# One gathered pair in fp32, fourteen early weight slots, and expert outputs fetched back by row index

## Chip, cores and metric

The kernel runs on one core of a Trainium2 chip. The metric is device microseconds of that core. The kernel is fp32 throughout: a sequence of 512 tokens of width 1024 goes through one layer, a hybrid mixer and then a mixture of experts.

## What is computed

The mixer (short convolution, sparse attention, gated delta rule) is not touched by the change; what matters is that its result `x + mixer(...)`, called x1 here, is the input of the expert stage. Of that stage the reference says, in short:

```python
lg = xt @ w_rg + b_rg                      # 4 groups
grp = argmax(lg); p_grp = softmax(lg)[grp]
le = (xt @ w_re + b_re)[group grp]         # 8 experts in the group
top_p, top_i = top_k(softmax(le), 2)
gate = top_p / sum(top_p) * p_grp
expert = grp * 8 + top_i                   # 2 of 32 experts for each token
y = (silu(xb @ w_eg[e]) * (xb @ w_eu[e])) @ w_ed[e]    # for every expert's tokens xb
x = x1 + sum over a token's two experts of gate * y
```

`xt` is the normalised x1. An expert has three matrices of 1024 x 512 or 512 x 1024 in fp32, 2 MB each, and 512 tokens make 1,024 assignments, 32 for an expert on average. The kernel gives each expert 64 slots (`CAP`) and has a slow loop behind the main part for experts with more.

## The kernel before

Tokens lie in four tiles of 128 (`NT`), x1 in the tiles `x1p`. The order of the instructions on each engine is fixed when the program is built: a planner simulates the program and orders it by when things are ready; each engine's queue then runs in that order, with semaphores for the waits. Only the tags of tiles (which buffer is used again by what) and a few `issue_after` bounds are written by hand.

**The end of the mixer, lines 854 to 1022.** The product with `w_out` is made in column blocks: three quarters of the columns first (L864 to L874, sums in `acc` and `acc2`, added to x1 at L908 and L910), the last quarter tile by tile in the loop of L965 (products L973 to L975, added at L979). In the same loop each tile is routed: squares on ScalarE (L926), mean on VectorE (L984), the power -1/2 on GpSimd (L985), logits from transposed x1 (L940), and then a chain of some 17 short operations on VectorE (L1004 to L1018) that finds the group, the two experts and the mask `asg`. `slots_of` counts each token's place in its expert by a product with a triangular matrix (L961) and `choose` (L954) turns the places into a one-hot matrix `pm0`: token by slot, for the four experts of pairs 0 and 1.

**Pairs of experts.** The expert stage goes over 16 pairs; pair p holds experts p and p + 16, with 64 slots each, so 128 slots. The inputs of a pair are `xT`, 128 slots turned and scaled by the norm's gain. There are two ways to get it. For pairs 0 and 1 the tokens are gathered by TensorE: x1 is split into a rounded part `h2h` and a rest `h2l` (`parts`, a cast on VectorE at L921 and a subtraction on GpSimd at L922), and both are multiplied with the one-hot columns (`gather_t`, L1092 and L1093; 64 products of 256 columns), and the sums in four PSUM banks are scaled in 16 operations (L1129). The slots' token number, norm and gates come from another product (L1123) into `info0`. For pairs 2 to 15 `next_input` reads rows of x1 from device memory by an indirect DMA from GpSimd (L1137, out-of-range slots skipped), and TensorE turns them (L1144). The row indices `tix` come from a table written by eight indirect DMAs (L1064), read back by eight DMAs on ScalarE's queue (L1100) and summed at L1102.

**Weights.** `wchunk` (L1079) loads weights in pieces of 128 x 2048 fp32, 1.049 MB, on SyncE's queue (L1085), 12 a pair: four for the gate and up halves of each expert, two for its down half. A piece goes into the next of 18 slots in rotation, and its load waits until the slot's last user is done. The first 11 slots (`wslots`, L854) are free before the mixer ends; their loads are bound behind the loads of the mixer's last weights. The other seven (L1075, L1076) are the operand tiles of the `w_out` product, `hTh` and `hTl`, and the three tiles that held `h2h` and part of `h2l`.

**A pair's work.** `ffn_up` makes gate and up products for one expert (L1162 and L1163, side by side in the two column halves of the array), then silu and gating (L1173, L1174) and four transposes (L1180, copied at L1181). `ffn_down` makes the down products (L1206). What happens to the output depends on the pair:

- Pairs 0, 2, ..., 12 (`by_rows`, L1260): the output is copied and scattered by an indirect DMA into `yrows` in device memory (L1215), at the row of its token, choice 1 and choice 2 apart. `yrows` was zeroed long before.
- The other pairs: the output is split in two parts (L1195, L1196) and combined by products with a one-hot matrix `sel` (L1240, 16 products a pair), whose sums are added to x1 on VectorE (L1242). These steps are strewn into the next pair's products (`combine_step`).

`add_rows` (L1223), called in pair 14, reads `yrows` back in eight plain DMAs of 0.5 MB on GpSimd's queue (L1227) and adds each to x1 (L1229). Its tiles `yr` share two buffers (`ringa`, tag `raw`) with the rows `xg` of `next_input`. The last expert's down half is loaded and combined in three column pieces (L1297 to L1313), each followed by the stores of these columns.

Of the kernel before, what the change touches and what calls it, by code (L numbers as in the profile page):

```python
# [11 lines left out]
F32 = mybir.dt.float32  # L12
# [87 lines left out]
def kernel(ctx, tc, x, w_in, w_nat, w_small, w_gate, w_branch, w_out, cmp_w1, cmp_w2,  # L100
# [753 lines left out]
    wslots = [(lp, "yg"), (mp, "es0"), (mp, "es1"), (lp, "nq"), (lp, "nkv")] + [(mp, f"es{i}") for i in range(2, 8)]  # L854
# [37 lines left out]
    tg = mp.tile([P, NT, 2, 4], F32, name="tg")  # L892
# [6 lines left out]
    G.tensor_copy(ti[:, :, 0], C("tokm"))  # L899
    for i in range(2):  # L900
        G.tensor_copy(inf[:, :, i, 0], C("tokm"))
        G.tensor_copy(tg[:, :, i, 0], C("tokm"))
        G.tensor_scalar(out=inf[:, :, i, 3], in0=C("tokm"), scalar1=float(S * i), scalar2=None, op0=ALU.add)
# [11 lines left out]
    def turned(ap, cols):
        return ap.rearrange("p (k q) -> p k q", k=KT)[:, :, cols.start // KT:cols.stop // KT]

    def parts(t, cols):
        x1 = x1p[t // 2][:, t % 2, cols].rearrange("p (q k) -> p k q", k=KT)
        hi, lo = turned(h2h[t // 2][:, t % 2], cols), turned(h2l[t], cols)  # L920
        V.tensor_copy(hi, x1)  # L921
        G.tensor_tensor(out=lo, in0=x1, in1=hi.bitcast(F32), op=ALU.subtract)  # L922
# [21 lines left out]
    for t in range(NT):  # L944
# [3 lines left out]
        parts(t, c3[0])  # L948
    pm0 = [lp.tile([P, 2, 4, CAP], F32R, tag=f, name="pm0") for f in ("fa", "fb")]


    def choose(pm, t):
        for b in range(2):
            V.tensor_tensor(out=pm[t // 2][:, t % 2, 2 * b:2 * b + 2],  # L954
                            in0=iota[:, 1:1 + CAP].unsqueeze(1).to_broadcast([P, 2, CAP]),
                            in1=pos[:, t, b::16].unsqueeze(2).to_broadcast([P, 2, CAP]), op=ALU.is_equal)
# [8 lines left out]
    for t in range(NT):  # L965
# [53 lines left out]
        parts(t, c3[1])  # L1019
# [18 lines left out]
    A.activation(exs, exs, AF.Exp)  # L1038
    V.tensor_reduce(out=se, in_=ex, axis=AX.X, op=ALU.add)
# [36 lines left out]
    slots += [(lp, "yhi"), (lp, "ylo"), (mp, "h2lp")]  # L1076
# [13 lines left out]

    def gather_t(px, k, t, sel, start, stop):
        T.matmul(px, h2h[t // 2][:, t % 2, k * P:(k + 1) * P], sel, start=start, stop=False)  # L1092
        T.matmul(px, h2l[t][:, k * P:(k + 1) * P], sel, start=False, stop=stop)  # L1093
# [331 lines left out]
```

## Time and profile before

| what | value |
|---|---|
| median of 3 runs (lowest, highest) | 1220.06 us (1218.9, 1220.84) |
| the profiled execution: time | 1220.9 us |
| the profiled execution: span | 1219.1 us |
| mean granted TensorE clock | 0.965 |
| PE, DVE, ACT, POOL busy | 91%, 48%, 27%, 10% of the span |
| moved by DMA | 274.81 MB, mean 225 GB/s |

The profile shows one execution on the chip. PE is TensorE's products, PEld its weight loads, DVE VectorE, ACT ScalarE, POOL GpSimd, SP SyncE; an engine's name with a q is its queue, which issues DMAs. L1162 is line 1162 of the kernel before. A row of a timeline has start and duration in us, engine and line, operation, the output and inputs by their names in the program, and a count where neighbours are merged; in square brackets stands how long the engine had been idle before it, and what ended that. A row of a list of waits has the sum, the number and the longest. Matrix products are pipelined, so a busy PE need not be at its peak. What a product costs is read from the distance between starts.

### The profile page before, as it was taken

To read this page: it belongs to the slowest core of one execution; us is meant where nothing else is said; L and a number is where in the kernel's file an instruction comes from. 1 tells how busy PE (TensorE), PEld (TensorE's weight loads), DVE (VectorE), ACT (ScalarE), POOL (GpSimd) and SP (SyncE) were. 2 spreads that over 40 slices of the span, in tenths; PEclk is the share of its full clock that TensorE was granted. 3 is DMA by queue.
4 is the path that set the end of the run, shared out by engine and by line. 5 is a ranking of instruction groups with operands and counts; after the bars stand their busy time and mean duration, and the time that the engine had idled before them with its cause. 6 is when DMAs were issued, how large, how long until landed. Compare 5 with 4: busy or idle time off the path is not lost. (4 is left out here: it accounts for less than half of the span.)

```text
span 1219.1 us, 15948 instructions
## 1 busy us (share of the span) xinstructions
PE 1115.0 (91%) x6167; PEld 717.7 (59%) x6168; DVE 590.3 (48%) x1406; ACT 332.3 (27%) x640; POOL 117.1 (10%) x172
## 2 busy tenths in 40 slices
PE   0899999999999999999999889997997989797985
PEld 0788798987788887766889833433332323232333
DVE  1586585586544775564445842414141414141356
ACT  1434343343332544566234201010110101010110
POOL 3100220410010000000002431000010000000000
PEclk9899999999999999999999889999998989898997
DMA  8133233212213221200781679999999999999953
GB/s 328 56 101 90 70 104 124 93 62 87 70 53 114 87 71 51 55 16 13 257 328 74 242 274 418 420 418 419 419 418 420 420 420 419 419 419 418 412 215 122
DMA packets 53488, 274.81 MB, mean 225 GB/s; under 512 B 8500, under 2 KB 12468, under 8 KB 28576
## 3 DMA queue, kind: packets, MB, share of 16 engines
q1 hardware_dynamic: 44928, 254.95, 53.8%
q0 software_dynamic: 5328, 14.33, 3.1%
q10 hardware_dynamic: 3152, 4.45, 1.0%
q8 instruction: 50, 0.82, 0.3%
q14 instruction: 30, 0.25, 0.1%
HBM read 266.73 MB, written 12.34 MB: 229 GB/s over the span
## 5 line engine op out<-in xcount | busy, mean ns | idle before, releaser
L1162 PE MATMUL pgu<-we,xT 128*64 128x512 f32 x512 | 245.1, 627 | 37.8 <-DMA we<-in_w_eg_dram 29.1
L1163 PE MATMUL pgu<-we,xT 128*64 128x512 f32 x512 | 240.6, 619 | 4.5 <-DMA we<-in_w_eu_dram 4.4
L189 PE MATMUL pmm<-hTh,lo 128*128 128x512 f32 x432 | 172.0, 398 | 0.2 <-DVE lo L182 0.2
L187 PE MATMUL pmm<-hTh,hi 128*128 128x512 f32 x432 | 171.2, 396 | 0.0
L188 PE MATMUL pmm<-hTl,hi 128*128 128x512 f32 x432 | 170.9, 395 | 0.0
L182 DVE TENSOR_TENSOR lo<-raw,hi 128x1024 fp32r<-128x1024 f32 x82 | 100.9, 1231 | 115.6 <-ACT hi L181 113.3
L1162 PEld LDWEIGHTS pgu<-we,xT 128*64 128x64 f32 x512 | 69.8, 143 | 130.2 <-issue 105.9
L181 ACT CAST hi<-raw 128x1024 fp32r<-128x1024 f32 x82 | 86.1, 1050 | 165.5 <-PE pmm L188 94.9
L1206 PE MATMUL pd<-we,aT 128*64 128x512 f32 x496 | 122.3, 598 | 0.5 <-DVE aT L1181 0.5
L1163 PEld LDWEIGHTS pgu<-we,xT 128*64 128x64 f32 x512 | 69.5, 142 | 63.2 <-issue 48.8
L1173 ACT ACTIVATE act<-pgu,rss 64x512 f32<-64x512 f32 x32 | 21.8, 681 | 274.0 <-PE pgu L1163 181.4
L189 PEld LDWEIGHTS pmm<-hTh,lo 128*128 128x128 f32 x432 | 81.6, 189 | 17.9 <-DVE lo L182 1.8
L187 PEld LDWEIGHTS pmm<-hTh,hi 128*128 128x128 f32 x432 | 81.8, 189 | 16.6 <-DVE fa L704 0.6
L188 PEld LDWEIGHTS pmm<-hTl,hi 128*128 128x128 f32 x432 | 81.6, 189 | 16.5
L1174 DVE SCALAR_TENSOR_TENSOR act<-pgu,gsl,act 64x512 f32<-64x512 f32 x32 | 24.2, 757 | 128.0 <-ACT act L1173 127.7
L1181 DVE COPY aT<-pt 128x256 f32<-128x256 f32 x32 | 13.5, 423 | 127.8 <-PE pt L1180 127.8
L1206 PEld LDWEIGHTS pd<-we,aT 128*64 128x64 f32 x496 | 35.5, 136 | 60.8 <-issue 56.1
L1240 PE MATMUL pc<-y,sel 128*128 128x512 f32 (+2 forms) x152 | 51.6, 450 | 10.5 <-DVE x L1242 6.4
L1242 DVE TENSOR_TENSOR x<-pc,x 128x512 f32<-128x512 f32 (+2 forms) x76 | 46.0, 656 | 22.4 <-PE pc L1240 21.8
L1240 PEld LDWEIGHTS pc<-y,sel 128*128 128x128 f32 x152 | 26.3, 198 | 44.5 <-DVE y L1196 14.4
L1195 ACT CAST y<-pd 64x512 fp32r<-64x512 f32 (+2 forms) x40 | 21.2, 537 | 104.5 <-PE pd L1206 53.6
L1215 POOL DMA_INDIRECT yrows<-yd,yix x14 | 14.2, 1013 | 274.6 <-ACT yd L1214 266.8
(794 smaller groups left out, 1849.4 us busy)
## 6 DMA issues: line engine op xcount, KB each, us to landing
we<-in_w_eg_dram SPq DMA_DIRECT2D x64, 1024.0 KB, 20.6
we<-in_w_eu_dram SPq DMA_DIRECT2D x64, 1024.0 KB, 20.0
we<-in_w_ed_dram SPq DMA_DIRECT2D x62, 1024.0 KB, 20.9
raw<-in_w_in_dram SPq DMA_DIRECT2D x30, 512.0 KB, 3.5
raw<-in_w_gate_dram SPq DMA_DIRECT2D x24, 512.0 KB, 3.5
raw<-in_w_branch_dram SPq DMA_DIRECT2D x12, 512.0 KB, 3.5
yrows<-zero POOLq DMA_DIRECT2D x1, 4096.0 KB, 21.7
raw<-in_w_nat_dram SPq DMA_DIRECT2D x8, 512.0 KB, 4.1
```

The lines of the kernel that those rows point to most:

```text
L181: A.copy(out=hi, in_=raw)
L182: V.tensor_tensor(out=lo, in0=raw, in1=hi.bitcast(F32), op=ALU.subtract)
L187: T.matmul(ps, ahi(k), bhi(k), start=start and k == 0, stop=False)
L188: T.matmul(ps, ahi(k), blo(k), start=False, stop=False)
L189: T.matmul(ps, alo(k), bhi(k), start=False, stop=stop and k == n - 1)
L1162: T.matmul(pgu[0:64], xs(k), wg(k), start=k == 0, stop=k == KT - 1)
L1163: ins = T.matmul(pgu[64:128], xs(k), wu(k), start=k == 0, stop=k == KT - 1)
L1173: A.activation(at, qk(pgu[0:64]), AF.Silu, scale=rss[0:64])
L1174: V.scalar_tensor_tensor(out=at, in0=qk(pgu[64:128]), scalar=gsl[64:128], in1=at, op0=ALU.mult, op1=ALU.mult)
L1206: T.matmul(pd[64 * a:64 * a + 64], aT[:, k], wd(k, a), start=k == 0, stop=k == 3)
L1240: T.matmul(pc[:, 0:n], sel[:, t * P:(t + 1) * P], y[:, cols], start=i == 0, stop=i == len(src) - 1)
L1242: V.tensor_tensor(out=xo, in0=pc[:, 0:n], in1=xo, op=ALU.add)
```

## The change

1. **Gather.** Only pair 0 is gathered by TensorE, and in fp32 straight from x1: 32 products of 128 columns, no split. `parts` and its buffers `h2h`, `h2l`, `h2lp` go; the squares are written to a plain tile `sq`; `choose` and `tg` cover two experts in place of four. The sums lie in two PSUM banks; one is scaled by one VectorE operation, the other by four on ScalarE. The slots' information for pair 0 is made inside pair 0's first up half (`first_info`). Pair 1's rows are now fetched by `next_input` like the others'.
2. **Slots.** `h2lp` is gone, and a tile `es8` of the same size is added. It and the tiles `yhi` and `ylo`, used before by `h2h`, are now among the early slots: 14 early ones in place of 11, and 18 in all as before.
3. **Outputs.** Pairs 0 to 6 are scattered in place of 0, 2, ..., 12; pairs 7 to 15 are combined by products. `add_rows` is called in pair 8. It computes row indices, sets assignments to later pairs out of range, and fetches `yrows` by eight indirect DMAs into zeroed tiles.
4. The activation table for silu is loaded once behind the exponentials of the routing.

```diff
-    wslots = [...] + [(mp, f"es{i}") for i in range(2, 8)]
+    wslots = [...] + [(mp, f"es{i}") for i in range(2, 9)]
+    wslots += [(lp, "yhi"), (lp, "ylo")]
...
-    h2h = [lp.tile([P, 2, D], F32R, tag=t, name="h2h") for t in ("yhi", "ylo")]
-    h2l = [ringa.tile([P, D], F32R, tag="raw", name="h2l", bufs=2) for _ in range(2)]
-    h2lp = mp.tile([P, 2, D], F32R, tag="h2lp", name="h2lp")
-    h2l += [h2lp[:, t] for t in range(2)]
+    sq = ringa.tile([P, D], F32, tag="raw", name="sq", bufs=2)
...
-        A.activation(turned(h2l[t], cols), x1.rearrange("p (q k) -> p k q", k=KT), AF.Square, accum_out=ss)
+        A.activation(sq[:, cols], x1p[t // 2][:, t % 2, cols], AF.Square, accum_out=ss)
...
-        parts(t, c3[0])
-    pm0 = [lp.tile([P, 2, 4, CAP], F32R, tag=f, name="pm0") for f in ("fa", "fb")]
+    pm0 = [lp.tile([P, 2, 2, CAP], F32, tag=f, name="pm0") for f in ("fa", "fb")]
...
-        for b in range(2):
-            V.tensor_tensor(out=pm[t // 2][:, t % 2, 2 * b:2 * b + 2],
...
+        V.tensor_tensor(out=pm[t // 2][:, t % 2], in0=iota[:, 1:1 + CAP].unsqueeze(1).to_broadcast([P, 2, CAP]),
+                        in1=pos[:, t, 0::16].unsqueeze(2).to_broadcast([P, 2, CAP]), op=ALU.is_equal)
...
-        parts(t, c3[1])
...
+    A.activation(sc[:, 63:64], mhalf, AF.Silu)
...
-    slots += [(lp, "yhi"), (lp, "ylo"), (mp, "h2lp")]
...
+    row2 = lambda t: pm0[t // 2][:, t % 2].rearrange("p e s -> p (e s)")
+    pxs = [mpsum(n).rearrange("p (i n) -> p i n", i=4) for n in ("pgu", "pd")]
     for t in range(NT):
         for k in range(KT):
-            gather_t(pxs[k // 2][:, k % 2], k, t, row4(pm0, t), t == 0 and k % 2 == 0, t == NT - 1 and k % 2 == 1)
...
-    inputs = [pair_input() for _ in range(2)]
-    for b, xT in enumerate(inputs):
-        for k in range(KT):
-            V.tensor_scalar(out=xT[:, k], in0=pxs[k // 2][:, k % 2, P * b:P * b + P], scalar1=gain[:, k:k + 1],
-                            scalar2=None, op0=ALU.mult)
+            T.matmul(pxs[k // 4][:, k % 4], x1p[t // 2][:, t % 2, k::KT], row2(t), start=t == 0 and k % 4 == 0,
+                     stop=t == NT - 1 and k % 4 == 3)
+    inputs = [pair_input()]
+    V.tensor_tensor(out=inputs[0][:, 0:4], in0=pxs[0], in1=gain[:, 0:4].unsqueeze(2).to_broadcast([P, 4, P]), op=ALU.mult)
+    for k in range(4, KT):
+        A.activation(inputs[0][:, k], pxs[1][:, k - 4], AF.Copy, scale=gain[:, k:k + 1])
+    info0 = mp.tile([P, 4], F32, name="info0")
+
+    def first_info(h):
+        if h == 0:
+            pi = ps_e.tile([P, 4], F32, tag="pt", name="pi")
+            for t in range(NT):
+                T.matmul(pi, row2(t), tg[:, t], start=t == 0, stop=t == NT - 1)
+            V.tensor_copy(info0, pi)
+        return slot_info(info0, slice(64 * h, 64 * h + 64), 2 + h)
...
-        if pair < 4:
+        if pair < 3:
             G.memset(xg, 0.0)
...
     def add_rows():
+        rix = mp.tile([P, NT, 2], I32, name="rix")
+        V.tensor_scalar(out=half, in0=at_e, scalar1=float(by_rows), scalar2=4096.0, op0=ALU.is_ge, op1=ALU.mult)
+        V.scalar_tensor_tensor(out=half, in0=half, scalar=4096.0, in1=over, op0=ALU.add, op1=ALU.add)
+        V.tensor_tensor(out=rix, in0=half, in1=inf[:, :, :, 3], op=ALU.add)
         for i in range(2):
             for t in range(NT):
                 yr = ringa.tile([P, D], F32, tag="raw", name="yr", bufs=2)
-                G.dma_start(yr, yrows[2 * S * i + 2 * P * t:2 * S * i + 2 * P * t + 2 * P].rearrange("(p a) n -> p (a n)", a=2))
+                G.memset(yr, 0.0)
+                G.indirect_dma_start(out=yr, out_offset=None, in_=yrows.rearrange("(r a) n -> r (a n)", a=2),
+                                     in_offset=bass.IndirectOffsetOnAxis(ap=rix[:, t, i:i + 1], axis=0),
+                                     bounds_check=2 * S - 1, oob_is_err=False)
                 x1 = x1p[t // 2][:, t % 2]
                 V.tensor_tensor(out=x1, in0=yr, in1=x1, op=ALU.add)
...
-    by_rows = range(0, 14, 2)
...
-                     None if h else up[1][0], yix[:, h, pair:pair + 1] if pair in by_rows else None)
+                     None if h else up[1][0], yix[:, h, pair:pair + 1] if pair < by_rows else None)
...
-            if h == 0 and pair == by_rows[-1] + 2:
+            if h == 0 and pair == by_rows + 1:
                 add_rows()
```

More of the change, by code (lines that the diff above doesn't have):

```diff
@@ L851 @@
     branch(1, yhi, ylo)
-    wslots = [(lp, "yg"), (mp, "es0"), (mp, "es1"), (lp, "nq"), (lp, "nkv")] + [(mp, f"es{i}") for i in range(2, 8)]
+    wslots = [(lp, "yg"), (mp, "es0"), (mp, "es1"), (lp, "nq"), (lp, "nkv")] + [(mp, f"es{i}") for i in range(2, 9)]
+    wslots += [(lp, "yhi"), (lp, "ylo")]
     m_hi, m_lo = quarters("hTh", F32R), quarters("hTl", F32R)
@@ L891 @@
     inf = mp.tile([P, NT, 2, 4], F32, name="inf")
-    tg = mp.tile([P, NT, 2, 4], F32, name="tg")
+    tg = mp.tile([P, NT, 4], F32, name="tg")
     exi = mp.tile([P, NT, 2], F32, name="exi")
@@ L899 @@
     G.tensor_copy(ti[:, :, 0], C("tokm"))
+    G.tensor_copy(tg[:, :, 0], C("tokm"))
     for i in range(2):
         G.tensor_copy(inf[:, :, i, 0], C("tokm"))
-        G.tensor_copy(tg[:, :, i, 0], C("tokm"))
         G.tensor_scalar(out=inf[:, :, i, 3], in0=C("tokm"), scalar1=float(S * i), scalar2=None, op0=ALU.add)
@@ L913 @@
     c3 = slice(0, 768), slice(768, 1024)
[L915 to L922, printed above, removed]
     def squares(t, cols, ss):
-        x1 = x1p[t // 2][:, t % 2, cols]
-        A.activation(turned(h2l[t], cols), x1.rearrange("p (q k) -> p k q", k=KT), AF.Square, accum_out=ss)
+        A.activation(sq[:, cols], x1p[t // 2][:, t % 2, cols], AF.Square, accum_out=ss)
     x1T = [None] * NT
@@ L1046 @@
     V.tensor_tensor(out=oh[0], in0=oh[0], in1=oh[1], op=ALU.add)
+    G.tensor_copy(tg[:, :, 1], rs4)
+    G.tensor_copy(tg[:, :, 2:4], oh[0][:, :, 0::16])
     G.tensor_copy(ti[:, :, 1], rs4)
@@ L1089 @@
     gain = PR("nffg")
-    def gather_t(px, k, t, sel, start, stop):
-        T.matmul(px, h2h[t // 2][:, t % 2, k * P:(k + 1) * P], sel, start=start, stop=False)
-        T.matmul(px, h2l[t][:, k * P:(k + 1) * P], sel, start=False, stop=stop)
     def pair_input():
@@ L1111 @@
                             scalar2=8192.0 + a, op0=ALU.mult, op1=ALU.add)
-    row4 = lambda pm, t: pm[t // 2][:, t % 2].rearrange("p e s -> p (e s)")
-    pxs = [mpsum("pgu") for _ in range(2)] + [mpsum("pd") for _ in range(2)]
-    pxs = [px.rearrange("p (i n) -> p i n", i=2) for px in pxs]
+    row2 = lambda t: pm0[t // 2][:, t % 2].rearrange("p e s -> p (e s)")
+    pxs = [mpsum(n).rearrange("p (i n) -> p i n", i=4) for n in ("pgu", "pd")]
     for t in range(NT):
         for k in range(KT):
-            gather_t(pxs[k // 2][:, k % 2], k, t, row4(pm0, t), t == 0 and k % 2 == 0, t == NT - 1 and k % 2 == 1)
-    pi = ps_e.tile([P, 2, 4], F32, tag="pt", name="pi")
-    for b in range(2):
-        for t in range(NT):
-            T.matmul(pi[:, b], row4(pm0, t)[:, P * b:P * b + P].bitcast(F32), tg[:, t, b], start=t == 0, stop=t == NT - 1)
-    info0 = mp.tile([P, 2, 4], F32, name="info0")
-    V.tensor_copy(info0, pi)
-    inputs = [pair_input() for _ in range(2)]
-    for b, xT in enumerate(inputs):
-        for k in range(KT):
-            V.tensor_scalar(out=xT[:, k], in0=pxs[k // 2][:, k % 2, P * b:P * b + P], scalar1=gain[:, k:k + 1],
-                            scalar2=None, op0=ALU.mult)
+            T.matmul(pxs[k // 4][:, k % 4], x1p[t // 2][:, t % 2, k::KT], row2(t), start=t == 0 and k % 4 == 0,
[12 more added lines that the diff above has]
+        return slot_info(info0, slice(64 * h, 64 * h + 64), 2 + h)
     def next_input(pair):
         xg = ringa.tile([P, D], F32, tag="raw", name="xg", bufs=2)
-        if pair < 4:
+        if pair < 3:
             G.memset(xg, 0.0)
@@ L1266 @@
             up.append(ffn_up(lambda k: xT[:, k, es], *weights_up(w_eg[e], w_eu[e]),
-                             lambda: slot_info(info0[:, pair], es, 2 + h) if pair < 2 else slot_info(info[:, pair], es),
+                             lambda: slot_info(info[:, pair], es) if pair else first_info(h),
                              up[0][0] if up else None))
```

5 lines of the change are left out of this document (1 added, 4 removed).

## The prediction

> **What bounds the kernel now.** I read the table by stages first: a row is a stretch, then the five engines' busy time and count, the granted TensorE clock, the share of the transfer engines and GB/s.
>
> ```profile
> 650.00:660.00 10.00, 10.00 (x85) 10.00 (x85) 3.83 (x4) 2.09 (x2) 0.00 (x0) 1.00 0.01 2
> 690.00:700.00 10.00, 7.44 (x48) 6.80 (x49) 8.26 (x50) 0.22 (x1) 2.29 (x4) 0.81 0.69 258
> 700.00:710.00 10.00, 4.60 (x29) 4.51 (x28) 6.05 (x32) 0.00 (x0) 6.68 (x9) 0.67 0.59 214
> 710.00:720.00 10.00, 9.58 (x40) 3.48 (x42) 5.78 (x28) 1.03 (x1) 3.75 (x4) 0.84 0.46 143
> 720.00:1150.00 430.00, 390.27 (x1711) 142.75 (x1707) 120.82 (x273) 44.46 (x73) 27.04 (x27) 0.95 1.01 419
> 1150.00:1180.00 30.00, 26.60 (x119) 10.42 (x119) 16.24 (x33) 2.95 (x6) 1.27 (x3) 1.00 0.71 270
> ```
>
> At 650 to 660 PE is full and the transfers idle. From 720 to 1150 it is the other way round: the transfer engines are full (1.01, 419 GB/s) and PE is not. What PE lacks there is told by its waits over 720 to 1186, longest first, and by its last long one:
>
> ```profile
> PE pgu L1162 <- DMA we<-in_w_eg_dram: 29.1, 5, 8.3
> ...
> 1106.13 1.94 PE L1162 MATMUL pgu<-we,xT 128*64 128x512 f32 x2 [5.42 <-DMA we<-in_w_eg_dram]
> ```
>
> So in the expert stage time is bytes over 419 GB/s, counted from the moment the stream can run. By the code a weight piece is 1.049 MB, 2.50 us; a pair of experts has 12, 30.0 us. PE needs less, as its timeline shows piece by piece:
>
> ```profile
> 1113.31 0.59 PE L1163 MATMUL pgu<-we,xT 128*64 128x512 f32 x1
> ...
> 1113.74 0.59 PE L1163 MATMUL pgu<-we,xT 128*64 128x512 f32 x1
> ...
> 1121.77 0.46 PE L1180 MATMUL pt<-c_ident,act 64*128 64x64 f32 x4
> ...
> 1152.72 3.65 PE L1206 MATMUL pd<-we,aT 128*64 128x512 f32 x16
> ...
> 1156.31 2.24 PE L1240 MATMUL pc<-y,sel 128*128 128x512 f32 x8
> 1158.41 1.31 PE L1144 MATMUL pxg<-c_ident,xg 128*128 128x128 f32 x8
> ```
>
> A step of 0.43 us (1113.31 to 1113.74) holds one record of L1162 and one of L1163; an expert has 16 of each, 6.9 us for its up half, and 3.65 us for its down half. A pair costs 2 x (6.9 + 3.65) + 1.3 (turning the next rows) + 2 x 0.46 = 23.3 us, and 27.8 us when its 16 L1240 products (two runs of 2.24 us) are made too.
>
> The stream cannot run before pair 0 frees a weight slot. SP's timeline: the first weight issue, the last w_out load, the 18th weight and the 19th.
>
> ```profile
> 581.36 0.42 SPq L1085 DMA_DIRECT2D we<-in_w_eg_dram  x1
> ...
> 642.45 0.33 SPq L178 DMA_DIRECT2D raw<-in_w_out_dram  x1
> ...
> 703.04 0.38 SPq L1085 DMA_DIRECT2D we<-in_w_eu_dram  x1
> 715.45 0.33 SPq L1085 DMA_DIRECT2D we<-in_w_eg_dram  x1
> ```
>
> All 18 slots have been asked for at 703.04. The 19th piece goes out at 715.45, 5 us behind pair 0's first product, and so the remaining 174 pieces hang on pair 0's start. What that waits for is read backwards on PE, POOL, ACT and DVE:
>
> ```profile
> 682.88 0.28 PE L975 MATMUL pd<-hi,hTl 128*128 128x256 f32 x1
> ...
> 702.55 2.05 PE L1123 MATMUL pi<-tg,pm 128*128 128x4 f32 x16
> 710.42 1.08 PE L1162 MATMUL pgu<-we,xT 128*64 128x512 f32 x1 [5.82 <-issue]
> ```
> ```profile
> 673.92 3.47 POOL L922 TENSOR_TENSOR h2l<-x,h2h 128x768 fp32r<-128x768 f32 x2
> 677.36 0.57 POOL L985 TENSOR_TENSOR sc<-sc,mhalf 128x1 f32<-128x1 f32 x1
> ```
> ```profile
> 706.59 6.92 ACTq L1100 DMA_DIRECT2D xT<-islots  x8
> ```
> ```profile
> 677.96 0.26 DVE L1004 SCALAR_TENSOR_TENSOR rt<-pgu,sc,prm 128x36 f32<-128x36 f32 x1 [0.55 <-POOL sc L985]
> ...
> 685.07 0.42 DVE L979 TENSOR_TENSOR x<-pd,x 128x256 f32<-128x256 f32 x1
> ...
> 695.79 0.18 DVE L1018 TENSOR_TENSOR asg<-oh,oh 128x32 bf16<-128x32 f32 x1
> ...
> 698.42 0.49 DVE L954 TENSOR_TENSOR pm<-c_moe,pos 128x128 fp32r<-128x128 f32 x2
> ...
> 707.65 1.12 DVE L1129 TENSOR_SCALAR xT<-pgu,prm 128x128 f32<-128x128 f32 x4
> ...
> 710.75 1.11 DVE L1129 TENSOR_SCALAR xT<-pd,prm 128x128 f32<-128x128 f32 x4
> ```
>
> Routing of the first token tile begins on DVE at 677.96, because the power on POOL (L985, 677.36) stood behind subtractions of 3.47 us. Four tiles' routing then fills DVE (8.26 of 10 us in 690 to 700) until 695.79. The last gather on PE ends at 702.55, its information products at 704.60; DVE copies that, builds selections and scales 16 column blocks until 711.86. From gather to first product pass 7.9 us.
>
> At the other end the transfers are already part idle (0.71 in 1150 to 1180), and ACT and DVE show what is late:
>
> ```profile
> 1182.20 0.68 ACT L1173 ACTIVATE act<-pgu,rss 64x512 f32<-64x512 f32 x1 [11.97 <-PE pgu L1163]
> ...
> 1189.23 1.23 DVE L1229 TENSOR_TENSOR x<-yr,x 128x1024 f32<-128x1024 f32 x1 [2.72 <-DMA yr<-yrows]
> ...
> 1197.20 1.23 DVE L1229 TENSOR_TENSOR x<-yr,x 128x1024 f32<-128x1024 f32 x1
> ...
> 1205.07 0.32 DVE L1196 TENSOR_TENSOR y<-pd,y 64x160 fp32r<-64x160 f32 x1 [2.55 <-ACT y L1195]
> ...
> 1209.51 2.48 DVE L1242 TENSOR_TENSOR x<-pc,x 128x320 f32<-128x320 f32 x6
> ```
>
> The last up half is done at 1182.2. Then adds of fetched rows (L1229, eight of 1.23 us, six of them after 1182) share DVE with the combination, and themselves wait for fetches through two buffers. The last ends at 1198.4, the last combination (L1242) at 1212.0, the span at 1219.1.
>
> **The change, part by part.** The sum is made against the profiled execution, 1220.9 us (1219.1 of span and 1.8 around it), 0.8 above the median of the runs.
>
> *Start of pair 0.* PE's products for tile 3's last columns end at 683.2, and those stay; DVE can add them (L979) at about 683.5 in place of 685.07. Removed are eight casts on DVE, eight subtractions on POOL, one of two comparisons a tile (L954), and the 16 scalings with the information ahead of them. With POOL free, tile 0's routing can start near 674, when its logits are there. A routing chain is 17 DVE operations of 0.19 to 0.26 us (the rows of L1018 and L1004), 3.8 us. Tile 3's add at 683.5, its square, power and logits some 2.5 us, then 3.8 us alone or 7 mixed with tile 2's, give 690 to 693 for what ended at 695.97. From there to the end of the choice were 2.9 us (698.91), 1 if no other gather is ahead on PE: 691 to 696. The gather stays at 16 records a tile: 8 fp32 products, two records each, as the 8 products of L1123 show (x16), each 0.13 us (2.05/16); the old 16 took 3.6 us (698.91 to 702.55). So 2.1 to 3.6 us. One DVE operation over the 512 columns that four took 1.11 us for, beside four on ACT, scales the result: 1 us; pair 0's sums take buffers that are free already. That is 694 to 701; I take **697.5, 12.9 us earlier**. Late next is the information for pair 0's activation, now four small products behind its up half, covered by the second expert's 6.9 us.
>
> *Three early slots.* By themselves they shorten nothing. The three pieces (7.5 us) go behind the last w_out load at 642.45, where transfers idle (0.01), and the 15th to 18th when the old operand tiles come free near 683, so 18 lie in SBUF at about 694. Without them the last three would be issued as late as 703 and eat half of the gain: they are the cover of the first part.
>
> *Bytes in the stream.*
>
> ```profile
> q0 software_dynamic: 5328, 14.33, 3.1%
> ```
>
> The software queue's 14.33 MB are 4.19 of zeros, 0.26 of zeroed tables, 8 fetches of 0.524 = 4.19, and 5.69 for 14 gathers and 14 scatters that could hold 11.0: they are 52% full, 0.27 MB a gather and 1.9 MB the scatters. The new fetch moves those 1.9 MB inside the stream, pair 1's gather 0.27; of the old fetches one or two (0.5 to 1.0 MB) fell into it. Net 1.2 to 1.7 MB: **+3.5 us**. The scatters stay 14.
>
> *The tail.* With the rows added in mid-stage, behind 1182.2 stand only act and turn (2.5 us to the turned activation, 1185), the last down products, six y halves (0.32) and twelve adds (0.41 of 320 columns, 0.5 of 384; the last six took 2.48): 10 us on DVE with the first products ahead, so 1197 with gaps, and 7.1 us from the last add to the end. 22 us in place of 37: **-15**.
>
> *Mid-stage.* In pair 8 POOL zeroes and fetches eight tiles through two buffers that also carry the next pairs' rows. POOL works in order: pair 10's gather stands behind all eight. DVE's adds stand in DVE's order, with act, turns and xT behind them, and PE waits for those. An indirect fetch under the stream lands late, and POOL is busy with each:
>
> ```profile
> yr<-yrows POOLq DMA_DIRECT2D x8, 512.0 KB, 4.3
> ...
> xg<-x1rows,tix POOLq DMA_INDIRECT x14, 9.0
> ```
> ```profile
> 691.00 0.95 POOL L1136 MEMSET xg<- 128x1024 f32 x1 [2.38 <-PE pgu L1093]
> ...
> 1096.46 1.04 POOL L1137 DMA_INDIRECT xg<-x1rows,tix  x1 [0.30 <-issue]
> ```
>
> With 9.0 us to land, 2.0 to zero and issue and 1.2 to add, a buffer turns in 12.2 us: eight fetches by twos take 49 us, where about 30 pass until pair 10's rows are wanted. That is between nothing (planned far enough ahead) and 28 us of PE stall with the gather's landing; against it stand seven later pairs in which PE is 30.0 - 27.8 = 2.2 us quicker than the stream, 15 us. I take a net 0, nearest to the row of 2.2 us, and keep both ends. DMA: Bandwidth & Descriptors of the Trainium skill (Anatomy of one DMA) puts such a fetch at 2.0 us plus bytes at 436 GB/s, an estimate of 2.5 us here, by which a buffer would turn in 6 us and nothing would stall. The row of 9.0 us disagrees with it.
>
> *Load on PE.* Pairs 7 to 15 all make their L1240 products: 27.8 us against 30.0, still under the stream. With 10% of hitches it would be 30.5, worth 9 x 0.5 = 4 us. There may also be a gain: the transfers had idled 0.29 of 30 us by 1180, so up to 9 us go if arrivals pace PE to the end. I take 0, the stream's row.
>
> The sum: 1220.9 - 12.9 + 3.5 - 15.0 + 0 = **1196.5 us**.
>
> **The rivals.** *Paced by arrivals to the end:* 9 us less, 1187.5. For it: weights are PE's only long wait until 1106. Against it: the late pairs are all heavy ones. The skill's landing time would lead here too.
>
> *The refetch holds PE:* 28 us less 15 made good, 1209.5. The row of 9.0 us speaks for it, PE's spare time against.
>
> *The start does not move,* so the slots do nothing. Half of the new scaling is on ACT, whose queue also issues eight table loads (L1100, 706.59 to 713.51), each behind a scatter. Planned behind them, the scaling lets pair 0 start near 708: 1207. Against it: the scaling is ready some 5 us earlier, and order is planned by readiness.
>
> *Slower:* the fetches go one at a time, because a gather for a later pair holds one of the two buffers all along. 8 x 12.2 = 98 us from the middle of pair 8, pair 10's rows behind them, wanted after 43: with 9 to land a stall of 64, less 15, 1245. It decides from 24.4 + 15 = 39 us of stall on. The old fetches had such a queue (the add of 1189.23 had waited 2.72 us for one); that rows are turned before each pair speaks against it.
>
> **How the numbers follow.** Forecast (1189 to 1203) 0.48; paced by arrivals 0.17; refetch holds PE 0.15; start does not move 0.10; slower 0.08; two of the middle ones together, which cancel the gain, 0.02. The range runs from the paced case with a start at 694 and 2 us less in the tail, 1182, to the refetch case with 2.5 us more, 1212. About 0.2% (2.4 us) is what a measurement of this kernel can tell from no change. Faster 0.89, same 0.03, slower 0.08.
>
> **What would show it.** Pair 0's first L1162 within 694 to 701, and SP's 19th piece 5 us behind it; three pieces issued right behind the last w_out load; a transfer share of 1.01 from then to about 1150; POOL's eight fetches in pairs 8 and 9, and no L1229 in the last 150 us; an end 22 us behind the last up half. Wrong would be PE waits of over 15 us on rows or sums near pairs 9 and 10, ACT's scaling behind L1100, or a share under 1.0 in mid-stage, which would mean full slots and PE as the bound.
>
> Pair 0's first products (1.08 us at 710.42, not 0.59) ran at a lower clock (0.67 in 700 to 710). TensorE: Matmul & The Clock Gate of the Trainium skill (Part 1: The HAM clock gate) says the clock halves after an idle window of about 3.4 us, which the row bears out; by that rule a gap of 1 us would keep it up and save another 1.3 us (three steps of 0.43), which is not in the sum.

## The result, and the profile after

| kernel | median (lowest, highest) | ratio to the kernel before, 95% interval |
|---|---|---|
| before, measured beside it | 1219.62 us (1218.9, 1220.84) | |
| changed | 1236.14 us (1235.55, 1239.42) | 1.014 [1.012, 1.016] |

The change costs 16.5 us where 24 were to be gained. The profiled execution has a span of 1233.8 us (before 1219.1). The table by stages of the changed kernel, in the columns used above (line numbers, from here on, are those of each kernel's own text):

```profile
700.00:710.00 10.00, 10.00 (x47) 4.76 (x48) 0.86 (x2) 1.14 (x4) 7.13 (x8) 0.91 0.38 89
710.00:720.00 10.00, 7.92 (x36) 2.86 (x32) 0.31 (x2) 1.96 (x2) 0.84 (x1) 1.00 1.03 391
720.00:1150.00 430.00, 363.94 (x1572) 137.86 (x1574) 131.22 (x296) 40.24 (x65) 44.64 (x45) 0.92 0.98 399
1150.00:1180.00 30.00, 30.00 (x130) 11.81 (x126) 15.71 (x33) 3.69 (x6) 0.00 (x0) 1.00 1.01 412
```

From 720 to 1150 the transfers moved 399 GB/s where there were 419, and PE was idle for 66 of 430 us (before 40). From 1150 to 1180 it is the other way round: PE is full and does not wait. PE's waits over 720 to 1186:

```profile
PE pgu L1143 <- DMA we<-in_w_eg_dram: 22.8, 4, 6.6
PE pt L1161 <- DVE act L1155: 15.9, 7, 6.5
PE pxg L1125 <- DMA xg<-x1rows,tix: 8.8, 1, 8.8
PE pgu L1144 <- DMA we<-in_w_eu_dram: 7.5, 2, 6.6
```

Weights are still the longest wait (L1143 and L1144, 30.3 us). New are pair 0's activations (the longest wait for act, 6.5) and one wait of 8.8 us for rows. The start, on PE, ACT and DVE:

```profile
701.98 0.64 PE L1143 MATMUL pgu<-we,xT 128*64 128x512 f32 x1
...
724.39 0.69 PE L1161 MATMUL pt<-c_ident,act 64*128 64x64 f32 x4 [6.47 <-DVE act L1155]
730.98 3.68 PE L1187 MATMUL pd<-we,aT 128*64 128x512 f32 x8 [5.90 <-DVE aT L1162]
...
742.48 0.61 PE L1143 MATMUL pgu<-we,xT 128*64 128x512 f32 x1 [0.43 <-DVE xT L1126]
```

```profile
704.52 10.71 ACTq L1078 DMA_DIRECT2D xT<-islots  x7
715.35 1.28 ACT L1154 ACT_TABLE_LOAD   x1 [10.78 <-DMA islots<-inf,isl]
716.64 0.68 ACT L1154 ACTIVATE act<-pgu,rss 64x512 f32<-64x512 f32 x1
```

```profile
712.66 0.16 DVE L1110 COPY info<-pi 128x4 f32<-128x4 f32 x1 [11.76 <-PE pi L1109]
...
720.47 1.01 DVE L1080 TENSOR_REDUCE info<-xT 128x64 f32<-128x512 f32 x1 [7.47 <-DMA xT<-islots]
...
723.58 0.76 DVE L1155 SCALAR_TENSOR_TENSOR act<-pgu,gsl,act 64x512 f32<-64x512 f32 x1
...
725.49 4.06 DVE L1137 TENSOR_SCALAR tok<-info 64x1 f32<-64x1 f32 x24
```

Pair 0 starts at 701.98, 8.4 us earlier than before. Its information is there at 712.8, but ACT's queue issues seven more table loads until 715.2, each behind a scatter, and a load of the activation table (1.28 us) follows right ahead of the first silu. Part 4 was meant to spare that load, but its early silu (L1021) ran at 7.0 us, at the very start of the span, and the table was loaded again at 715.35. DVE has the table's sum (L1080, at 720.47 after a wait of 7.47) ahead of the gating product (723.58), and 24 token operations of 4.06 us ahead of the copy aT. PE waits 6.47 and 5.90 us, and pair 1 starts at 742.48. Before, pair 1's products filled such gaps, since its input lay there already; its first product in the kernel before:

```profile
726.04 0.64 PE L1163 MATMUL pgu<-we,xT 128*64 128x512 f32 x1
```

The refetch, on POOL, and what PE does behind it:

```profile
962.43 1.04 POOL L1216 DMA_INDIRECT yr<-yrows,rix  x1 [6.18 <-DMA yrows<-yd,yix]
984.50 0.95 POOL L1215 MEMSET yr<- 128x1024 f32 x1 [21.03 <-DVE x L1220]
...
1021.14 0.99 POOL L1216 DMA_INDIRECT yr<-yrows,rix  x1 [0.27 <-POOL yr L1215]
1023.14 0.99 POOL L1118 DMA_INDIRECT xg<-x1rows,tix  x1 [1.01 <-DVE x L1220]
```

```profile
1023.65 0.74 PE L1231 MATMUL pc<-y,sel 128*128 128x512 f32 x2 [1.69 <-DVE x L1233]
1033.21 1.94 PE L1125 MATMUL pxg<-c_ident,xg 128*128 128x128 f32 x8 [8.82 <-DMA xg<-x1rows,tix]
```

The gather for pair 10 (1023.14) stands behind all eight fetches, and PE waits 8.82 us for its rows. The end came as forecast; the last silu, on ACT:

```profile
1211.80 0.68 ACT L1154 ACTIVATE act<-pgu,rss 64x512 f32<-64x512 f32 x1 [10.25 <-PE pgu L1144]
```

It stands 22.0 us ahead of the end of the span (before 36.9).

The last weights for an up half were asked for at about the same time in both kernels, by the timeline of SP, before and after:

```profile
1162.53 1.00 SPq L1085 DMA_DIRECT2D we<-in_w_eu_dram  x1
```

```profile
1160.42 0.38 SPq L1067 DMA_DIRECT2D we<-in_w_eu_dram  x1
```

Before, the last silu followed 20 us later (1182.2), now 51 us later. So at the end PE is a whole stock of slots behind the stream (18 pieces of 2.50 us are 45 us): it has become the bound.

### The profile page after: what moved, and what is told of

Read it like the earlier page. It is cut to its first block, busy times and chain, and to the rows that moved or that the text cites. A ratio compares the mean times of both kernels' runs of the same rounds, so it can differ in the third digit from the quotient of the medians.

```text
span 1233.8 us, 15931 instructions
## 1 busy us (share of the span) xinstructions
PE 1119.9 (91%) x6167; PEld 723.9 (59%) x6168; DVE 575.7 (47%) x1384; ACT 332.7 (27%) x647; POOL 113.5 (9%) x170
## 3 DMA queue, kind: packets, MB, share of 16 engines
q0 software_dynamic: 5472, 11.29, 2.4%
## 5 line engine op out<-in xcount | busy, mean ns | idle before, releaser
L1143 PE MATMUL pgu<-we,xT 128*64 128x512 f32 x512 | 245.2, 625 | 23.5 <-DMA we<-in_w_eg_dram 22.8
L1144 PE MATMUL pgu<-we,xT 128*64 128x512 f32 x512 | 244.4, 624 | 7.5 <-DMA we<-in_w_eu_dram 7.5
L1143 PEld LDWEIGHTS pgu<-we,xT 128*64 128x64 f32 x512 | 69.1, 143 | 125.7 <-issue 98.3
L1187 PE MATMUL pd<-we,aT 128*64 128x512 f32 x496 | 127.1, 613 | 5.9 <-DVE aT L1162 5.9
L1154 ACT ACTIVATE act<-pgu,rss 64x512 f32<-64x512 f32 x32 | 21.8, 681 | 330.8 <-PE pgu L1144 293.1
L1144 PEld LDWEIGHTS pgu<-we,xT 128*64 128x64 f32 x512 | 67.0, 142 | 50.9 <-issue 40.3
L188 PEld LDWEIGHTS pmm<-hTl,hi 128*128 128x128 f32 x432 | 81.6, 189 | 16.5
L1126 DVE TENSOR_TENSOR xT<-pxg,prm 128x512 f32<-128x512 f32 x30 | 20.2, 689 | 70.3 <-PE pxg L1125 51.3
```

What stands on the lines that cost most here:

```text
L188: T.matmul(ps, ahi(k), blo(k), start=False, stop=False)
L1143: T.matmul(pgu[0:64], xs(k), wg(k), start=k == 0, stop=k == KT - 1)
L1144: ins = T.matmul(pgu[64:128], xs(k), wu(k), start=k == 0, stop=k == KT - 1)
L1154: A.activation(at, qk(pgu[0:64]), AF.Silu, scale=rss[0:64])
L1187: T.matmul(pd[64 * a:64 * a + 64], aT[:, k], wd(k, a), start=k == 0, stop=k == 3)
```

## The experiments

Three theories. **A, order**: scattered pairs leave PE idle beside a full stream, and combined pairs in a row take PE as long as the stream or longer, so the idle time is never made good. **B, refetch**: fetches in mid-stage stop PE. **C, start**: pair 0's activations behind the table loads and the table's sum lose what the gather gained.

| run | base and edit | median, us | ratio, 95% interval |
|---|---|---|---|
| undo_outputs | changed, part 3 undone | 1216.44 | 0.9981 [0.9971, 0.9990] |
| outputs_only | before, part 3 alone | 1239.31 | 1.0163 [1.0145, 1.0181] |
| no_refetch | changed, rows not fetched | 1232.19 | 1.0110 [1.0089, 1.0131] |
| tables_late | changed, table loads behind silu | 1239.47 | 1.0173 [1.0152, 1.0194] |
| order_only | undo_outputs, pairs 0 to 6 scattered | 1249.16 | 1.0246 [1.0229, 1.0263] |
| light_last | undo_outputs, pairs 7 to 13 scattered | 1239.93 | 1.0172 [1.0155, 1.0189] |
| tables_pool | undo_outputs, table loads on POOL | 1211.79 | 0.9933 [0.9916, 0.9949] |
| six_scattered | undo_outputs, 0 to 10 scattered, refetch in pair 12 | 1232.81 | 1.0116 [1.0099, 1.0133] |
| all_combined | tables_pool, nothing scattered | 1248.54 | 1.0251 [1.0223, 1.0278] |
| spread_raw | tables_pool, 0 to 10 scattered, one fetch at a time | 1228.88 | 1.0088 [1.0059, 1.0116] |
| spread_own | spread_raw, own buffers | 1214.22 | 0.9963 [0.9949, 0.9977] |
| six_own | tables_pool, 0 to 10 scattered, block of fetches, own buffers | 1222.45 | 1.0030 [1.0015, 1.0044] |
| two_gathered | tables_pool, pair 1 gathered by TensorE too | 1221.08 | 1.0018 [1.0005, 1.0031] |

Each ratio is to the kernel before, measured beside it (1219.5 to 1219.8 us). A second table follows the stage through the second silu of some pairs (timeline of ACT, us), the activation behind the pair's second up half and so a mark of how far PE has come, and the tail behind the last one (span less that silu):

| kernel | pair 4 | pair 8 | pair 10 | pair 15 | tail |
|---|---|---|---|---|---|
| before | 829.0 | 956.8 | 1019.0 | 1182.2 | 36.9 |
| undo_outputs | 834.4 | 951.5 | 1014.4 | 1179.4 | 33.5 |
| order_only | 827.2 | 975.0 | 1046.7 | 1204.4 | 41.4 |
| no_refetch | 829.3 | 974.7 | 1048.1 | 1209.1 | 21.8 |
| changed | 828.2 | 970.2 | 1057.9 | 1211.8 | 22.0 |
| light_last | 851.6 | 982.6 | 1029.6 | 1194.3 | 44.0 |
| tables_pool | 833.2 | 952.2 | 1017.9 | 1186.1 | 24.5 |
| six_scattered | 834.1 | 951.7 | 1014.5 | 1204.2 | 26.1 |

### Which part of the change costs

```diff
-    by_rows = 7
+    by_rows = range(0, 14, 2)
...
-                     None if h else up[1][0], yix[:, h, pair:pair + 1] if pair < by_rows else None)
+                     None if h else up[1][0], yix[:, h, pair:pair + 1] if pair in by_rows else None)
...
-            if h == 0 and pair == by_rows + 1:
+            if h == 0 and pair == by_rows[-1] + 2:
                 add_rows()
```

> Base: the changed kernel (1236.1 us), with part 3 taken back: pairs 0, 2, ..., 12 are scattered again and fetched back by plain DMAs in pair 14; gather and slots stay as changed. Theory A (order: nine heavy pairs in a row at the end, light ones whose spare PE time is wasted at the front) and theory B (the refetch in mid-stage stalls PE by some 13 us) both put the loss into part 3: 1212 to 1222, at or a little under the kernel before (1219.6), with transfers full until about 1150. Theory C (pair 0's activations stand behind the table loads on ACT's queue and the table's sum on DVE, some 15 us of idle PE before pair 1, so that the stream runs 8 us later than before) puts it into the first part: 1226 to 1236, with the first product of pair 1 at about 740 as in the changed kernel.

outputs_only puts the reverse of this diff, with the indirect fetches, into the kernel before.

> Base: the kernel before (1219.6 us), with part 3 alone: pairs 0 to 6 scattered, refetch by eight indirect fetches in pair 8; the old gather of two pairs and the old slots. Theories A and B: 1228 to 1240, with a PE stall of 10 us or more near pair 10 and PE without waits on weights from about 1040. Theory C alone: part 3 would give its shorter tail, about 1205, since nothing of pair 0 changes.

Part 3 costs 19.7 us on top of the other parts (1236.14 - 1216.44) and 19.9 without them (1239.31 - 1219.45). The parts add up: the others gain 3.0 us, part 3 loses 20. That speaks for A or B and against C as the cause of the loss.

### Order or refetch

```diff
-            if h == 0 and pair == by_rows + 1:
-                add_rows()
```

> Base: the changed kernel (1236.1 us) without the refetch: the rows of pairs 0 to 6 are scattered, but neither fetched nor added, so their addition is left out. Theory B (the stall of the refetch is lost for good, since PE is the bound behind it): 13 to 18 us less, 1218 to 1223. Theory A alone (the order costs, the refetch only fills time in which PE would wait for weights): 1231 to 1236, with PE's idle time moved to waits for weights.

```diff
-    by_rows = range(0, 14, 2)
+    by_rows = range(7)
...
-            if h == 0 and pair == by_rows[-1] + 2:
+            if h == 0 and pair == 14:
                 add_rows()
```

> Base: undo_outputs (1216.4 us); one edit: pairs 0 to 6 are scattered in place of 0, 2, ..., 12. The refetch stays as before, plain DMAs in pair 14. Theory A (a combined pair costs PE as much as the stream brings, about 30 us, so nine of them in a row never catch up, and PE ends one slot stock behind the stream): last silu at about 1207 to 1210 as in no_refetch, then the old tail of 30 us or more behind it, 1238 to 1250. Theory B (order costs nothing, the refetch in mid-stage is what costs): 1214 to 1222.

Without the refetch 3.9 us go, not 13 to 18. The order alone costs 32.7 us (1249.16 - 1216.44), with the same fetches called in the same pair; in the profiled executions 24.9 of it stand at the last silu and 7.9 in the tail. B falls as the main cause. Where the order loses is shown by two long stretches, undo_outputs first, order_only second:

```profile
740.00:980.00 240.00, 221.17 (x984) 85.03 (x982) 73.88 (x169) 24.46 (x40) 16.29 (x16) 0.96 1.01 418
980.00:1180.00 200.00, 178.44 (x780) 63.98 (x776) 61.29 (x130) 20.75 (x34) 11.94 (x14) 0.96 0.97 395
```

```profile
740.00:980.00 240.00, 196.82 (x862) 74.57 (x863) 33.82 (x79) 18.90 (x30) 21.10 (x21) 0.92 1.01 414
980.00:1180.00 200.00, 193.38 (x813) 73.01 (x813) 93.52 (x189) 24.49 (x41) 6.94 (x8) 0.99 0.98 396
```

Up to 980 the transfers are full in both (1.01), but PE did 221 us of work in the one and 197 in the other. The combination's products alone (L1223), from 690 to 980, in the same two kernels:

```profile
690.00:980.00 290.00, 21.10 (x64) 10.54 (x64) 0.94 0.95 386
```

```profile
690.00:980.00 290.00, 0.00 (x0) 0.00 (x0) 0.90 0.94 380
```

These 21 us fill PE's gaps in alternating order and do not exist yet in a row of scattered pairs; they are most of the 24 us that PE still owes at 980. Behind 980 PE is busy for 193 of 200 us and has nothing to pay with. At pair 8 order_only is 23.5 us late (975.0 against 951.5), at the last silu 25.

```diff
-    by_rows = range(0, 14, 2)
+    by_rows = range(7, 14)
```

> Base: undo_outputs (1216.4 us); one edit: pairs 7 to 13 are scattered in place of 0, 2, ..., 12; plain refetch in pair 15. The work is that of order_only in the reverse order: combined pairs first. Theory A: the combined pairs then run beside a full stream, the scattered ones catch up the stock behind it, and PE is close behind the last arrivals again: last silu at 1176 to 1186, 1212 to 1224 in all (the refetch comes a pair later, so the tail may be up to 8 us longer). Rival (any run of equal pairs costs, since PE's spare time in scattered pairs is lost wherever they stand in a row): like order_only, 1235 or more.

By its time the rival of this run held (1235 or more), and theory A's last silu at 1176 to 1186 did not come. Combined pairs first take 33 us each (second silu of pair 1 at 759.7, of pair 7 at 958.1), the slots fill, the stream falls to 388 GB/s in 740 to 980, and the scattered pairs behind can't run ahead of it: the last silu is 15 us late. A further 10.5 us stand in the tail, where the fetches come a pair later than in undo_outputs, so this row costs less than that of order_only. But it costs: it is not only that combined pairs stand last. In these rows the slower of PE and stream sets the pace, where alternation lets the mean of two pairs count.

### What a combined pair costs

```diff
-    by_rows = range(0, 14, 2)
+    by_rows = ()
...
-            if h == 0 and pair == by_rows[-1] + 2:
-                add_rows()
```

> Base: tables_pool (1211.8 us); no pair is scattered and nothing is fetched back: all 16 pairs are combined by products. It measures what a combined pair costs PE when there is no other order to choose. Price of the prediction (27.8 us): the stream stays the bound with some 2 MB less to move, last silu at 1174 to 1182, then a tail of 22 to 25: 1197 to 1206. Price read from the changed kernel's last pairs (153.9 us for five, 30.8 each, up to 33 in light_last): pair 15's second silu 14 x 30.8 to 33 us behind pair 1's (756), 1187 to 1218, and 1210 to 1242 in all, with transfers below 1.0 in places because slots are full.

The result, 1248.54, lies above both ranges. The first silu of pairs 13 and 14 on ACT, then PE's waits and the stretch of five pairs that ends with the second:

```profile
1147.17 0.68 ACT L1155 ACTIVATE act<-pgu,rss 64x512 f32<-64x512 f32 x1 [13.58 <-PE pgu L1145]
...
1181.14 0.68 ACT L1155 ACTIVATE act<-pgu,rss 64x512 f32<-64x512 f32 x1 [13.58 <-PE pgu L1145]
```

```profile
PE pc L1225 <- DVE y L1179: 9.3, 15, 0.7
PE pt L1163 <- DVE act L1156: 7.8, 5, 1.6
PE pc L1225 <- DVE x L1227: 1.1, 5, 0.2
```

```profile
1011.34:1181.14 169.80, 151.61 (x640) 55.99 (x640) 66.56 (x138) 18.42 (x30) 2.98 (x3) 1.00 0.96 377
```

```profile
1011.34:1181.14 169.80, 27.98 (x80) 13.09 (x80) 1.00 0.96 377
```

A combined pair takes 34.0 us, over and over, with no wait for weights: 151.6 / 5 = 30.3 of products, and 18.2 / 5 = 3.6 of waits on a ring of PE, ACT and DVE (y halves before a combination, act before a turn). The third fence is PE as a whole, the fourth the combination's products alone: 28.0 / 5 = 5.6 us a pair, not 4.5. The 4.5 came from two runs of eight; here they are strewn in ones, twos and sixes. Waits and strewn products together make 27.8 + 3.6 + 1.1 = 32.5; what the last 1.5 us are is not shown.

### The refetch where PE has time to spare

```diff
-    by_rows = range(0, 14, 2)
+    by_rows = range(0, 12, 2)
```

> Base: undo_outputs (1216.4 us); one edit: pairs 0, 2, ..., 10 are scattered, the plain refetch in pair 12, pair 12 combined. It takes the refetch and its eight adds out of the tail, as the change meant to, without nine combined pairs in a row (four at the end). Theory A: last silu 0 to 5 us later than the 1179.4 of undo_outputs, and a tail of about 22 us in place of 33: 1204 to 1214. Theory B (a refetch in mid-stage costs PE 10 us or more): 1216 to 1226.

At 1232.81 it lies above both ranges. The tail falls by 7 us, but the last silu is 25 us late: here theory B holds. The order is not the reason, though five combined pairs stand in a row at the end (11 to 15, not four): spread_own below has the same row and takes 1214.22. The stall has one place: the second silu of pair 12 is at 1077.9, as in undo_outputs (1078.4), that of pair 14 at 1176.6 in place of 1142.9.

```diff
-                yr = ringa.tile([P, D], F32, tag="raw", name="yr", bufs=2)
+                yr = mp.tile([P, D], F32, tag="yr", name="yr", bufs=2)
```

> Base: tables_pool; pairs 0, 2, ..., 10 scattered, the eight fetches in one block in pair 12 as in six_scattered, but through two buffers of their own (17 weight slots). If the stall of six_scattered comes from the two shared buffers (rows of the next pair wait for a buffer): it goes, 1203 to 1212. If it comes from POOL's order (the next pair's gather is queued behind all eight fetches) or from the adds on DVE: the stall stays, 1222 to 1230, and the gather of pair 13 or 14 is issued behind the last fetch.

Own buffers took a part: pair 14's second silu is at 1164.2, 20 us behind the 1144.6 of its base tables_pool, where six_scattered lost 34 on its own base. The last gather now stands ahead of the last six fetches, so POOL's order does not explain the rest. POOL, DVE, and PE's longest wait in six_own:

```profile
1091.16 1.27 POOL L1119 DMA_INDIRECT xg<-x1rows,tix  x1 [44.71 <-PE pxg L1126]
1097.85 0.56 POOL L1212 DMA_DIRECT2D yr<-yrows  x1 [5.42 <-DVE x L1214]
```

```profile
1123.05 1.23 DVE L1214 TENSOR_TENSOR x<-yr,x 128x1024 f32<-128x1024 f32 x1 [7.29 <-DMA yr<-yrows]
1124.31 1.29 DVE L1227 TENSOR_TENSOR x<-pc,x 128x512 f32<-128x512 f32 x2
```

```profile
PE pc L1225 <- DVE x L1227: 12.6, 3, 6.8
```

DVE waits 7.29 us for a fetch to land, with the combination's additions (L1227) queued behind that one addition (L1214), and PE waits for these, 12.6 us. So the order on DVE carries a late fetch into PE; that is read from these rows, and no run has another order on DVE alone.

```diff
-            if h == 0 and pair == by_rows[-1] + 2:
-                add_rows()
+            if pair >= 12:
+                add_row()
+                if pair == 15:
+                    add_row()
```

> Base: tables_pool (1211.8 us); pairs 0, 2, ..., 10 are scattered as in six_scattered, but the eight tiles are fetched back and added one at a time, one behind each down product of pairs 12 to 14 and two at the end of pair 15, through the same two buffers that carry the next pairs' rows. In six_scattered the fetches in one block stopped PE (second silu of pair 14 at 1176.6 in place of 1142.9). Theory B (the block of fetches ahead of the next pair's rows stalls PE): the stall goes, last silu at 1180 to 1190, tail 22 to 28, 1203 to 1214. If the buffers themselves are what costs, taken one at a time too: 1216 to 1226.

> Base: spread_raw; the fetched tiles get two buffers of their own, and for their room there are 17 weight slots in place of 18 (es8 is left out). If the shared buffers cost, 4 to 10 us less than spread_raw; if not, the same within 2 us, or 1 to 3 us more for the slot.

Taken one at a time through the shared buffers the rows still cost 17 us over tables_pool, above both ranges; with own buffers 2.4, a gain of 14.7 where 4 to 10 were expected. So both count: fetches apart from each other, and buffers that the next rows don't need. Neither beats alternation with the fetch at the end.

### The start

tables_late moves the table loads behind the first silu and the table's sum behind the second gating product, and leaves out the unread token operations; tables_pool does so on undo_outputs, with the loads on POOL:

```diff
-        nc.scalar.dma_start(itab[:, j], tab.rearrange("(p e) c -> p (e c)", p=P))
+        nc.gpsimd.dma_start(itab[:, j], tab.rearrange("(p e) c -> p (e c)", p=P))
...
+        with tc.issue_after(marks[1][1]):
             V.tensor_reduce(out=info.rearrange("p e c -> p (e c)"), ...)
```

> Base: the changed kernel (1236.1 us), with three edits at pair 0: ACT's table loads behind the first silu, the table's sum and the indices on DVE behind pair 0's second gating product, and the 26 token operations of the scattered pairs (whose result nobody reads) left out. Theory C: pair 0's first gating product at about 713 in place of 723.6, pair 1's first product at 728 to 732 in place of 742.5, and 10 to 14 us less at the end, 1222 to 1226. Theory A alone (PE's heavy pairs set the end, with room ahead of them that takes up whatever is gained at the start): 1232 to 1236, with longer waits for weights in the light pairs.

> Base: undo_outputs (1216.4 us), where PE stops for some 11 us in pair 0 (silu at 715.5 behind the table loads, gating at 723 behind the table's sum). Edits: the table loads on POOL's queue, the table's sum and the indices on DVE behind pair 0's second gating product, no token operations for scattered pairs. Theory C (the start's gain is lost at pair 0's activations): first gating product at 713 to 715, second at 718 to 719, down products of pair 0 done by 728, pair 1's first product 3 to 8 us earlier than the 738 of undo_outputs (its rows hang on scatter, table and gather now), and since this order is bound by the stream, 3 to 8 us less, 1208 to 1214. If pair 0 has room: 1215 to 1218.

tables_late gained nothing (1239.47, above both ranges): the loads wait for their scatters and held the second silu until 725.3. tables_pool is 4.7 us faster than undo_outputs and the fastest kernel here, 7.7 us under the one before. But not for theory C's reason. PE at pair 0 in undo_outputs and in tables_pool:

```profile
723.78 0.69 PE L1161 MATMUL pt<-c_ident,act 64*128 64x64 f32 x4 [7.32 <-DVE act L1155]
728.29 3.30 PE L1187 MATMUL pd<-we,aT 128*64 128x512 f32 x8 [3.83 <-DVE aT L1162]
...
738.81 0.61 PE L1143 MATMUL pgu<-we,xT 128*64 128x512 f32 x1 [0.43 <-DVE xT L1126]
```

```profile
719.76 1.94 PE L1189 MATMUL pd<-we,aT 128*64 128x512 f32 x8 [0.52 <-DVE aT L1164]
...
734.89 1.97 PE L1126 MATMUL pxg<-c_ident,xg 128*128 128x128 f32 x8 [7.50 <-DMA xg<-x1rows,tix]
...
739.10 1.12 PE L1144 MATMUL pgu<-we,xT 128*64 128x512 f32 x1
```

Pair 0's waits (7.32 and 3.83) are gone, and in their place PE waits 7.50 us for pair 1's rows, which hang on scatter, table and gather. Pair 1 starts at 739.1 in place of 738.8. At pairs 4 to 10 the two kernels stand within 4 us, undo_outputs ahead at 8 and 10. The gain appears at the end: the last silu 6.6 us later, the tail 9.0 shorter. Seven of the eight adds of fetched rows stand ahead of the last silu in tables_pool (the first at 1160.4), three in undo_outputs (the first at 1172.5), which fits the shorter tail. Why the end came out so is not settled; the edits also gave all later work another order.

```diff
+        with tc.issue_after(marks[1][2]):
+            for t in range(NT):
+                for k in range(KT):
+                    T.matmul(px[k // 4][:, k % 4], x1p[t // 2][:, t % 2, k::KT], row2(t, 1), ...)
```

> Base: tables_pool (1211.8 us), where PE waits 7.5 us for pair 1's fetched rows (727.4 to 734.9) and pair 1's first products run at 1.06 us in place of 0.59. Edit: pair 1 is gathered by TensorE in fp32 too, 32 products bound behind pair 0's up halves; its rows are not fetched. If the rest of the start's missing gain hangs on pair 1's rows (scatter, table, gather): pair 1's first product at 733 to 737 in place of 739.1, no step at 1.06 us behind it, and 2 to 6 us less in all, 1206 to 1210. If the 8 us of additional products (32 of 0.26) eat what the wait gives: 1210 to 1214. More than 1214 would mean that the products stand ahead of pair 0's down halves and hold the slots.

PE behind pair 0's up halves in two_gathered:

```profile
721.75 2.64 PE L1120 MATMUL pxg<-pm,x 128*128 128x128 f32 x10
...
724.71 13.12 PE L1120 MATMUL pxg<-pm,x 128*128 128x128 f32 x54
737.76 1.94 PE L1202 MATMUL pd<-we,aT 128*64 128x512 f32 x8
```

The time, 1221.08, is the last case of the expectation (over 1214). Pair 1's 32 products are 64 records and take 15.8 us, not 8, and most stand ahead of pair 0's down products, which begin at 737.8 in place of 719.8 and free their slots that much later: the price for the wait of 7.5 us was twice the wait. Bound behind pair 0's first down half they might pay; that was not tried.

## Why the prediction was wrong

The sum was -12.9 (start) + 3.5 (bytes) - 15.0 (tail) + 0 (mid-stage) + 0 (load on PE). The runs split it in another way: -3.0 for the parts besides the outputs, +32.7 for the order, -13.0 for taking the fetches from pair 14 into pair 8, by row index (1236.14 - 1249.16). Tail and mid-stage together came within 2 us of their -15.0, in part by luck: the tail of order_only, from which the -13.0 is counted, is 41.4 us and not the 36.9 of the kernel before.

- **Load on PE: the step that failed**, 0 in place of 32.7. It said "27.8 us against 30.0, still under the stream". Alone in a row a combined pair takes 34.0, and the changed kernel's last five took (1211.8 - 1057.9) / 5 = 30.8 (why less than 34.0 is not settled), while the stream brought a pair in 31 (second silu of pairs 5 and 8: 877.1, 970.2). Two errors: the price was added up from products in runs, without the 3.6 us of waits and the higher price of strewn products; and the case "With 10% of hitches it would be 30.5, worth 9 x 0.5 = 4 us" counted only what a pair takes beyond the stream. What counts is that PE was left 24 us of work behind by the scattered pairs. The prediction's own sign for this, a transfer share under 1.0 in mid-stage with PE as the bound, came: 0.98 over 720 to 1150.
- **Mid-stage**: 0, as the net of a stall and "seven later pairs in which PE is 30.0 - 27.8 = 2.2 us quicker than the stream". The stall is there (8.8 us on rows, under the 15 that were named as a sign, and POOL's eight fetches in a row, as written), the making good is not. It costs 3.9 us in this order: without the refetch pair 9 came later (second silu at 1020.9, not 1011.1), so part of the time was lost elsewhere; why is not settled. By DMA: Bandwidth & Descriptors of the Trainium skill (Anatomy of one DMA), the estimate was 2.5 us for a fetch (of the 0.24 MB that the prediction gives it) and no stall. This trace disagrees, as the row of 9.0 us did before: the table of DMA issues has 8.5 here:

```profile
yr<-yrows,rix POOLq DMA_INDIRECT x8, 8.5
```

- **Start**: pair 0 at 697.5 was forecast, 701.98 came: the last tile's gather began at 697.89, behind a choice that was to end by 691 to 696, and took 4.1 us (16 records, to 701.98), not 2.1 to 3.6. The larger miss is what lay behind: "Late next is the information for pair 0's activation ... covered by the second expert's 6.9 us". The information was there at 712.8. What the step left out is that silu stands behind the table loads on ACT's queue and gating behind the table's sum on DVE, and that pair 1, no longer gathered, hangs on the table. The rival on ACT's queue looked at the scaling alone. Part 4 spared nothing: the activation table was loaded in front of that silu all the same, and the gating product came last anyway.
- **Slots**: as written: three pieces right behind the last w_out load, the 19th at 705.66, 3.7 us behind the first product.
- **Tail**: right, 22.0 us behind the last silu, for the reason given: no_refetch and all_combined, which add no fetched rows, have 21.8. But tables_pool comes within 2.5 us of it with the fetches still in pair 14.
- **Bytes**: +3.5 us was not measured by itself. The software queue moved 11.29 MB in all, where the prediction's parts give 14.33 - 4.19 + 1.9 + 0.27 = 12.3.
- **Rivals**: the one on the other side named fetches one at a time. It is the right side for the wrong reason: they went out over 59 us (962.4 to 1021.1), not 98. No rival had the row of equal pairs, though the prediction has the prices for its first half: 23.3 against 30.0 is 6.7 us of PE time lost in each scattered pair of a row.

## What to carry to other kernels

Where light and heavy stages share one stream, price the sequence and not the stage: in this kernel a row of equal stages took the larger of the two paces (31 us where the stream set it, 31 to 34 where PE did), and the alternation of undo_outputs 30.8 us a pair (second silu of pairs 4 and 14: 834.4, 1142.9), near the stream's 30.0. Take the price of a stage from a stretch in which it repeats, waits included, not from the sum of its products. Where an early operation is dropped, look for what it covered: here a second pair's ready input had been filling the first pair's gaps.

## What the runs showed of the hardware

- An fp32 product of 128 x 128 by 128 columns is two records of some 0.25 us each: 64 records in 15.8 us. The eight of a tile's gather took 4.1 us, 0.51 each.
- A wait of 6 us costs PE more than the 6 us. PE of the changed kernel in a scattered pair:

```profile
863.99 1.11 PE L1143 MATMUL pgu<-we,xT 128*64 128x512 f32 x1 [5.94 <-DMA we<-in_w_eg_dram]
864.90 1.06 PE L1143 MATMUL pgu<-we,xT 128*64 128x512 f32 x1
865.75 1.06 PE L1143 MATMUL pgu<-we,xT 128*64 128x512 f32 x1
```

The steps behind the wait are 0.85 us apart in place of 0.43, six of them, so this wait costs 2.5 us more. TensorE: Matmul & The Clock Gate of the Trainium skill (Part 1: The HAM clock gate) has the clock halved after an idle window of about 3.4 us. The trace agrees in the halving behind a wait of 5.94 us; it does not show where the limit lies. These waits fall where PE has time to spare; that they cost little in all is argued and was not measured.
